# Twenty column chunks of x's projections, computed in pairs by Strassen's product in a dense stage ahead of the mixers; first branch projection woven with the memory attention

## The chip, the cores and the metric

The kernel runs on one core of one Trainium2 chip. The metric is the device time of one execution in microseconds (us). A profile is one execution recorded by the hardware profiler; its engines are PE (TensorE matmul), PEld (TensorE weight load), DVE (VectorE), ACT (ScalarE), POOL (GpSimd) and SP (SyncE, which issues most DMAs).

## The reference, cut to what matters

One residual block over 1024 tokens of width 1024, everything in f32:

```python
h = rmsnorm(x, norm_mix_g)
hq, hf, hi, hg, fq, fk, fv, ff, mq, gate_logits = split(h @ w_in)
y_a = hgrn2_mixer(hq, hf, hi, hg)            # 4 heads x 128, chunkwise recurrence
y_b = fox_mixer(fq, fk, fv, ff)              # 8 heads x 64, causal attention with forget bias
y_c = memory_mixer(mq, rmsnorm(mem) @ mem_kv_w)   # 4 heads x 128, 256 memory tokens
g = sigmoid(gate_logits)                     # 3 branches x 1024 channels
merged = g[0] * (y_a @ w_br_hgrn) + g[1] * (y_b @ w_br_fox) + g[2] * (y_c @ w_br_mem)
x = x + merged @ w_out
x = x + conv_glu_ffn(rmsnorm(x))             # 2 x 2816 wide up, 1024 down
```

## The kernel before, in words

Activations lie channel-major: 128 channels on the partitions, 1024 tokens along the free axis, eight such k-blocks for width 1024. Every f32 matrix product is made of three fp32r matmuls (`mm3`, lines 109 to 111): each operand is split into a high part and a low part (`split`: an ACT cast, line 115, or a POOL cast, line 119, and a DVE subtraction, line 123), and high*high, high*low and low*high are added up in PSUM.

A **chunk** is 128 output columns of one of x's projections: `cm_chunk` loads a 128x1024 weight tile (`raw`, line 134, on SP's queue, two buffers), splits it, and runs for each half of the tokens 8 k-blocks x 3 matmuls of 128x512, 48 matmuls in all. The stationary operand is the weight tile, the moving one uh/ul, the two parts of x times the norm gain. Of these chunks there are 12 for the recurrence (hq, hf, hg; three a head, `hgrn_prep`), 4 for the memory queries (`mem_prep`, line 799) and 24 for the merge gates. A gate chunk is evicted by `gate`: a DVE multiply by the norm factor rx (line 373), an ACT tanh (line 374) and a store to a DRAM tile `gd` (line 388), from which the branch stage loads it again.

The order of the work:

1. Start: x and mem come in, uh/ul are made, the memory keys and values and the first two gate chunks are computed while x arrives.
2. `fox_values`, `fox_proj(0)`: token-major projections, matmuls of 128x256.
3. Attention (fox): passes p = 0 to 3 of two heads each. `weave` interleaves a head's steps (`ahead` gives them priority 300) with `fox_proj(p+1)` and with gate chunks, by the list `NGF` (13 in all); in pass 3 the filler is `hgrn_values`. `fox_prep` (line 475 on) transposes the next pass's queries and keys. The attention itself: two matmuls for the logits (lines 521, 522), a DVE pass that adds the bias and takes the maximum (527), exp on ACT (537), a reciprocal on DVE (538), a scaling on POOL (539), transposes on PE (550 to 553), a split, two matmuls (562, 563).
4. Recurrence (hgrn): `hgrn_prep(0)` alone, then `hgrn_mix(h)` woven with `hgrn_prep(h+1)` and gate chunks by `NG[0:4]` = 1, 1, 0, 3.
5. Memory attention: `mem_prep(0)` alone, then `mem_attn(h)` woven with `mem_prep(h+1)` and gate chunks by `NG[4:8]` = 0, 0, 0, 3.
6. Branches 1, 0, 2 (`gates`, `br_chunk`): eight chunks of 24 matmuls each; then w_out, then the ConvGLU, whose up-projection already goes by Strassen's product (`unit`: two chunks of 128 columns by seven block products of 4 k-blocks x 3 matmuls, 84 matmuls) and the down-projection likewise.

The order on each engine is fixed before the run by the framework's scheduler, which lists instructions by priority and by its own estimate of when their inputs are ready; on the chip each engine then runs its list in order.

Of the kernel before, what the change touches and what calls it, by code (L numbers as in the profile page):

```python
# [14 lines left out]
P = 128  # L15
# [18 lines left out]
FOX_LATE, MEM_LATE = 0.2, 0.3  # L34
# [31 lines left out]
def tile_block(ctx: ExitStack, tc: tile.TileContext, xT, memT, vec, fbias, mats, hmask, w_cm, w_hi, w_fqk, w_fv,  # L66
               w_mkv, w_br, w_out, w_up, w_dn, outT):
# [101 lines left out]
    order = [(br, j) for br in (1, 0, 2) for j in range(8)]  # L169
# [195 lines left out]
    gd = tc.dram_tile([NPRE, 2, P, HB], F32, name="gd")  # L365

    def gate_chunk(br, j):
        for n, ps in cm_chunk(w_cm[16 + 8 * br + j], KC, uh, ul):
            yield n, gate(n, ps)

    def gate(n, ps):
        gt = gp.tile([P, HB], F32, tag="gt", name="gt", bufs=3)
        V.tensor_mul(gt, ps, rx[:, n * HB:(n + 1) * HB])
        S.activation(gt, gt, AF.Tanh, scale=0.5)
        return gt
# [4 lines left out]
    early = iter(range(2, NPRE))  # L380

    def gates_early(count):
        for _ in range(count):
            i = next(early, None)
            if i is None:
                return
            for n, gt in gate_chunk(*order[i]):
                SP.dma_start(gd[i, n], gt)
                yield
# [215 lines left out]
    def hgrn_prep(h):  # L605
        ph = state["ph"]
        qt = ph.tile([P, T], F32, tag="hq", name=f"hq_{h}", bufs=2)
        at = ph.tile([P, T], F32, tag="ha", name=f"ha_{h}", bufs=2)
        gz = ph.tile([P, T], F32, tag="hz", name=f"hz_{h}", bufs=2)
        for what, base, dst in ((0, 4, at), (1, 0, qt), (2, 8, gz)):  # L610
            for n, ps in cm_chunk(w_cm[base + h], KC, uh, ul):
                sl = slice(n * HB, (n + 1) * HB)
                zt = ph.tile([P, HB], F32, tag="zt", name="zt")
                V.tensor_mul(zt, ps, rx[:, sl])
                d = dst[:, sl]
                S.activation(d, zt, AF.Tanh, scale=0.5)
                if what == 0:

                    G.tensor_scalar(d, d, TMIN, c1[:, h:h + 1], ALU.max, ALU.mult)
                else:  # L620

                    V.scalar_tensor_tensor(out=d, in0=d, scalar=1.0, in1=zt, op0=ALU.add, op1=ALU.mult)
                yield
        hset[h] = (qt, at, gz)

# [147 lines left out]
    yc = pyc.tile([P, 4, T], F32, tag="y16", name="yc")  # L773
    mkh = pm.tile([P, 4, NM], F32R, tag="mkh", name="mkh")
# [3 lines left out]
    mkf = pm.tile([P, 4, NM], F32, tag="mqh", name="mkf2", bufs=2)  # L778
    mvf = pm.tile([P, 2, HB], F32, tag="mql", name="mvf2", bufs=2)
    SP.dma_start(mkf.rearrange("p a b -> p (a b)"), kvd[:, 0, :])  # L780
    SP.dma_start(mvf.rearrange("p a b -> p (a b)"), kvd[:, 1, :])
    split(G, mkh, mkl, mkf)
    split(G, mvh, mvl, mvf)

    pyb = tc.alloc_tile_pool(name="pyb", bufs=1, side="left", reuse_waits="tile")
    yb = pyb.tile([P, 4, T], F32, tag="y16", name="yb")
    SP.dma_start(yb, ybd)
# [3 lines left out]
    def mem_prep(h):  # L791
        mqh = pm.tile([P, T], F32R, tag="mqh", name=f"mqh_{h}", bufs=2)
        mql = pm.tile([P, T], F32R, tag="mql", name=f"mql_{h}", bufs=2)
        rq = pm.tile([P, 8], F32, tag="rq", name=f"rq_{h}", bufs=2)
        prs = ps_tr()
        for n, ps in cm_chunk(w_cm[12 + h], KC, uh, ul):
            sl = slice(n * HB, (n + 1) * HB)
            sq = pm.tile([P, HB], F32, tag="msq2", name="msq2")
            S.activation(sq, ps, AF.Square)
            split(S, mqh[:, sl], mql[:, sl], ps)  # L800
# [3 lines left out]
            yield  # L804
# [4 lines left out]
        mset[h] = (mqh, mql, rq)  # L809

# [42 lines left out]
    wsplit[:] = [S, V]  # L853


    yts = {0: ya, 1: yb, 2: yc}

    spots = (("mqh", 2), ("mql", 2), ("mqh", 2), ("mql", 2), ("mkh", 1), ("mkl", 1), ("mvh", 1), ("mvl", 1))
    ys = [pm.tile([P, T], F32R, tag=t, name=f"y{i}", bufs=b) for i, (t, b) in enumerate(spots)]
    yh, yl = ys[0::2], ys[1::2]  # L860
    spots = (("msq2", 1), ("mpt", 3), ("mpt", 3), ("mpt", 3), ("mph", 2), ("mph", 2), ("mpl", 2), ("mpl", 2))
    mg0 = [pm.tile([P, HB], F32R if t in ("mph", "mpl") else F32, tag=t, name=f"mg0_{i}", bufs=b)
           for i, (t, b) in enumerate(spots)]
    mg1 = []

    def merged(j, n):
        return mg0[2 * j + n].bitcast(F32) if j < 4 else mg1[0][:, j - 4, n * HB:(n + 1) * HB]

    def br_chunk(br, j):


        wh, wl = weights(w_br[br, j], (4, P))
        half = [slice(n * HB, (n + 1) * HB) for n in range(2)]
        if j in (0, 7):
            get = ps_lg if j else ps_tr
            ps = [get(), get()]
# [11 lines left out]
    def gates():  # L888
        for i, (br, j) in enumerate(order):
            y = yts[br]  # L890
            gts = []
            if i < NPRE:
                for n in range(2):
                    gt = gp.tile([P, HB], F32, tag="gt", name="gt", bufs=3)
                    SP.dma_start(gt, gd[i, n])
                    gts.append(gt)
            else:
                gts = [gt for _, gt in gate_chunk(br, j)]
            if j == 0:
                for c in range(4):  # L900
                    split(S, yh[c], yl[c], y[:, c, :])
            if i == 4:
                mg1.append(pyb.tile([P, 4, T], F32, tag="y16", name="mg1"))
            for n, ps in br_chunk(br, j):
# [8 lines left out]
    run_all(gates())  # L913
    mh, ml = both_parts("m")
    for j in range(8):
        for n in range(2):
# [3 lines left out]
    pyb.release()  # L920
# [6 lines left out]

    pr = tc.alloc_tile_pool(name="pr", bufs=1, side="right", reuse_waits="tile")
    fam = {}

    def new_family(pool, name):
        fam[name] = [pool.tile([P, 4, HB], F32R, tag=f"{name}{p}", name=f"{name}{p}") for p in "hl"]

# [12 lines left out]
    def family_block(name, k, src):  # L946
        h, l = fam[name]
        return split(S, h[:, k, :], l[:, k, :], src)

# [5 lines left out]

    late = {}
# [77 lines left out]

    def product(ps, op, b, first):
        wh, wl = op
        bh, bl = fam[b]
        for k in range(4):
            ks = slice(k * P, (k + 1) * P)
            mm3(ps, wh[:, ks], wl[:, ks], bh[:, k, :], bl[:, k, :], first and k == 0, k == 3, not first)  # L1040
# [258 lines left out]
def _layout(inp):  # L1299
# [48 lines left out]
    o["w_cm"] = chunks(np.concatenate([hq, hf, hg, mq, gt], axis=1))  # L1348
# [44 lines left out]
```

## Time and profile before

| what | us |
|---|---|
| three runs, median (lowest to highest) | 1778.5 (1777.14 to 1780.22) |
| the profiled execution's own time | 1779.33 |
| its span, first to last instruction | 1777.6 |
| attention (fox) in the trace, first logits to last output | about 143.6 to 508 |
| recurrence (hgrn) | about 508 to 787 |
| memory attention | about 787 to 891 |
| branches and w_out | about 891 to 1123 |
| ConvGLU up, then down | about 1123 to 1554, then to the end |

The busy times of an engine are unions of its instructions' times. A matmul's recorded duration is its latency, about 400 ns for a 128x512 one, while successive ones start about 230 ns apart: a PE that is busy all the time may still run at full rate or not, and the rate is read from the number of matmuls in a stretch.

### The profile page before, as it was taken

How to read it: one execution, taken by the hardware profiler on the slowest of the kernel's cores; microseconds unless marked ns; L12 is line 12 of the kernel's file. 1: busy time of each engine (PE TensorE's matmuls, PEld its weight loads, DVE VectorE, ACT ScalarE, POOL GpSimd, SP SyncE). 2: the span in 40 equal slices, each digit the busy share in tenths (PEclk: the TensorE clock that was granted, in tenths of full speed). 3: DMA queues.
4: the chain of work that ended last, by engine and by line, in shares of the span. 5: the costliest groups of instructions: out<-in, count | busy, mean ns of one | idle time of the engine just before them, and what ended most of it. 6: DMA issues, size and time to landing. Idle time of an engine off the chain costs nothing.

```text
span 1777.6 us, 24366 instructions
## 1 busy us (share of the span) xinstructions
PE 1755.8 (99%) x9173; PEld 1487.1 (84%) x9173; DVE 1146.1 (64%) x2070; ACT 731.0 (41%) x1215; POOL 359.9 (20%) x430
## 2 busy tenths in 40 slices
PE   7999999999999999999999999999999999999999
PEld 5899899889988888888888888788888888778887
DVE  8436665565657778735446665787877877775654
ACT  4336454444544344314521143543433444433332
POOL 5214334342223333323100000111111111100000
PEclk9999999999999999999999999999999999999999
DMA  7212221221211111130144442455545444394782
GB/s 265 98 61 70 70 69 62 73 88 60 69 50 43 42 48 34 45 125 25 54 142 142 148 166 84 142 165 173 154 132 158 124 125 140 135 371 144 232 281 83
DMA packets 75573, 208.45 MB, mean 117 GB/s; under 512 B 8752, under 2 KB 11576, under 8 KB 75328
## 3 DMA queue, kind: packets, MB, share of 16 engines
q1 hardware_dynamic: 60864, 154.99, 25.2%
q0 software_dynamic: 14592, 51.91, 10.3%
q8 instruction: 72, 1.18, 0.3%
q14 instruction: 45, 0.37, 0.1%
HBM read 168.82 MB, written 61.12 MB: 129 GB/s over the span
## 4 chain that ended last, share of the span: by engine, by line
PE 96%; issue 1%; DMA 1%; DVE 1%; POOL 1%; ACT 0%; SPq 0%; DVEq 0%; POOLq 0%
PE pp L110 21%; PE pp L111 21%; PE pp L109 21%; PE lg L110 4%; PE lg L111 4%; PE lg L109 4%; PE tr L109 2%; PE tr L110 2%; PE tr L111 2%; PE lg L696 2%; PE po L563 1%; PE lg L522 1%; PE po L562 1%; PE lg L521 1%; PE po L110 1%
## 5 line engine op out<-in xcount | busy, mean ns | idle before, releaser
L111 PE MATMUL pp<-uh,wl 128*128 128x512 f32 x608 | 243.6, 401 | 0.0
L110 PE MATMUL pp<-ul,wh 128*128 128x512 f32 x608 | 243.2, 400 | 0.0
L109 PE MATMUL pp<-uh,wh 128*128 128x512 f32 x608 | 241.7, 397 | 0.0
L110 PE MATMUL pp<-wl,uh 128*128 128x256 f32 (+1 forms) x512 | 144.9, 283 | 0.0
L111 PE MATMUL pp<-wh,ul 128*128 128x256 f32 (+1 forms) x512 | 144.6, 283 | 0.0
L109 PE MATMUL pp<-wh,uh 128*128 128x256 f32 (+1 forms) x512 | 143.9, 283 | 0.0
L115 ACT CAST wh<-raw 128x1024 fp32r<-128x1024 f32 (+2 forms) x80 | 73.1, 914 | 153.0 <-PE pp L110 123.3
L109 PEld LDWEIGHTS pp<-uh,wh 128*128 128x128 f32 x608 | 115.3, 190 | 23.3
L110 PEld LDWEIGHTS pp<-ul,wh 128*128 128x128 f32 x608 | 114.5, 188 | 22.9
L111 PEld LDWEIGHTS pp<-uh,wl 128*128 128x128 f32 x608 | 114.4, 188 | 22.5
L1074 POOL DMA_DIRECT2D rw<-in_w_up x44 | 24.3, 559 | 463.8 <-DVE wl L123 410.8
L123 DVE TENSOR_TENSOR wl<-raw,wh 128x1024 fp32r<-128x1024 f32 (+2 forms) x87 | 93.9, 1081 | 29.7 <-ACT wh L115 23.0
L115 ACT CAST wh<-s 128x512 fp32r<-128x512 f32 x85 | 51.9, 619 | 125.6 <-PE pp L110 60.7
L110 PEld LDWEIGHTS pp<-wl,uh 128*128 128x128 f32 x512 | 96.4, 188 | 0.9
L111 PEld LDWEIGHTS pp<-wh,ul 128*128 128x128 f32 x512 | 96.5, 189 | 0.6
L109 PEld LDWEIGHTS pp<-wh,uh 128*128 128x128 f32 x512 | 96.2, 189 | 0.7
L115 ACT CAST dwh<-wr 128x1024 fp32r<-128x1024 f32 (+1 forms) x42 | 41.1, 980 | 124.7 <-PE tr L110 41.7
L115 ACT CAST wh<-rw 128x512 fp32r<-128x512 f32 x65 | 40.0, 620 | 86.1 <-PE pp L110 48.3
L123 DVE TENSOR_TENSOR dwl<-wr,dwh 128x1024 fp32r<-128x1024 f32 (+1 forms) x42 | 47.6, 1133 | 38.7 <-ACT dwh L115 37.5
L677 POOL TENSOR_TENSOR X<-X,kt 128x256 f32<-128x256 f32 x48 | 48.2, 1011 | 109.9 <-ACT X L676 109.9
L539 POOL TENSOR_SCALAR pt<-pt,st 128x128 f32<-128x128 f32 (+3 forms) x64 | 57.0, 891 | 62.4 <-DVE st L538 50.5
L537 ACT ACTIVATE pt<-pt,st 128x128 f32<-128x128 f32 (+3 forms) x64 | 49.7, 777 | 35.1 <-DVE st L534 29.0
(426 smaller groups left out, 4845.1 us busy)
## 6 DMA issues: line engine op xcount, KB each, us to landing
rw<-in_w_up POOLq DMA_DIRECT2D x44, 512.0 KB, 4.7
raw<-in_w_cm SPq DMA_DIRECT2D x40, 512.0 KB, 3.5
sd<-in_w_dn POOLq DMA_DIRECT2D x30, 512.0 KB, 6.1
br<-yd SPq DMA_DIRECT2D x30, 512.0 KB, 5.4
gd<-gt SPq DMA_DIRECT2D x46, 256.0 KB, 2.0
gt<-gd SPq DMA_DIRECT2D x46, 256.0 KB, 2.7
yd<-fc SPq DMA_DIRECT2D x44, 256.0 KB, 2.1
wr<-sd SPq DMA_DIRECT2D x20, 512.0 KB, 4.5
```

The costliest lines, as they stand in the source:

```text
L109: PE.matmul(ps, lh, rh, start=first, stop=False, skip_group_check=more)
L110: PE.matmul(ps, lh, rl, start=False, stop=False, skip_group_check=more)
L111: PE.matmul(ps, ll, rh, start=False, stop=last, skip_group_check=more)
L115: S.copy(out, in_)
L123: return (sub or V).tensor_sub(l, src, h.bitcast(F32))
L521: PE.matmul(ps[:, :w], qa[i][:, tsl], kh[i][:, s0:s0 + w], start=True, stop=False)
L522: fox_sets[p][3] = PE.matmul(ps[:, :w], qa[i][:, tsl], kl[i][:, s0:s0 + w], start=False, stop=True)
L537: S.activation(pt[:, :ns], pt[:, :ns], AF.Exp, bias=st[:, 2:3], accum_out=st[:, 3:4])
L539: G.tensor_scalar(pt[:, :ns], pt[:, :ns], st[:, 3:4], 0.0, ALU.mult, ALU.add)
L677: G.tensor_mul(Xk, Xk, Kv[:, :, 0, :])
L696: PE.matmul(o[:, b * 64:(b + 1) * 64], X[:, b * P:(b + 1) * P], Xq[:, b * bpb:(b + 1) * bpb, :], start=True, stop=True)
L1074: late["raw"] = G.dma_start(raw[:, 2 * i:2 * i + 2, :], src[:, 2 * i:2 * i + 2, :])
```

## The change: what it does

Ten **pairs** of chunks leave the mixers and are computed between the start and `fox_values`, each by seven products of half-size blocks instead of eight: (hf0, hq0), (hg0, a gate), the four memory-query chunks in two pairs, and twelve further gates in six pairs. That is the whole of `hgrn_prep(0)`, all of the projections of `mem_prep`, and 13 gate chunks. Two gate chunks (`NCOVER`) run ahead of them in the plain way. Three gate chunks stay with the attention, one each in passes 0 to 2; four stay with the recurrence (`NG` = 0, 1, 0, 3), none with the memory attention.

The Strassen blocks T1 to T4 are sums and differences of quarters of x, so x is read from memory a second time (`differences`, on POOL's DMA queue), scaled on ACT, and combined and split on DVE and ACT. The weights of a pair come in four quarters from a new input `w_pair` on POOL's queue. What the pairs give goes to DRAM tiles (`gd`, `hd`, `mqd`) and is loaded where it is used: `hgrn_load` takes the place of `hgrn_prep(0)`, and `mem_prep` loads its queries instead of projecting them.

The first branch (branch 1, the attention's) is woven with the memory attention; its input, the parts of y_b, lies in the tiles of uh/ul, which the last gate chunk, now run k-block by k-block, frees. Each branch's merged sums lie in other tiles than before.

```diff
-NGF = [0, 3, 1, 2, 0, 5, 2, 0]
-NG = [1, 1, 0, 3, 0, 0, 0, 3]
-NPRE = 2 + sum(NG) + sum(NGF)
+ORDER = [(br, j) for br in (1, 0, 2) for j in range(8)]
+NCOVER = 2
+NPAIR = 13
+NG = [0, 1, 0, 3]
+_dense = [4, 0, 8, 16 + 8 * ORDER[4][0] + ORDER[4][1], 12, 13, 14, 15]
+_dense += [16 + 8 * br + j for br, j in ORDER[5:4 + NPAIR]]
+PAIRS = list(zip(_dense[0::2], _dense[1::2]))
...
+    def product(ps, op, b, first):
+        wh, wl = op
+        for k in range(4):
+            ks = slice(k * P, (k + 1) * P)
+            bh, bl = block(b, k)
+            mm3(ps, wh[:, ks], wl[:, ks], bh, bl, first and k == 0, k == 3, not first)
...
+    def dense_unit(src, put, first, families):
+        raw = []
+        whole = None if first else dense.raw()
+        for i in range(2):
...
+            with tc.issue_after(late["rows"].ins):
+                G.dma_start(t, src[:, 2 * i:2 * i + 2, :])
+            raw += [t[:, 0, :], t[:, 1, :]]
+        a11, a21, a22, a12 = raw
+        x, y = ps_proj(), ps_lg()
+        o1 = dense.operand(a11)
...
+        product(x, o1, "B11", True)
+        e1 = dense.snap(x)
+        if first:
+            z = ps_tr()
+            product(z, o6, "B21", True)
+            put(0, 0, z, e1)
+            next(families)
+        product(y, o2, "T1", True)
+        e5 = dense.snap(y)
+        product(x, dense.operand(s2), "T2", False)
+        e2 = dense.snap(x)
+        run_all(families)
+        s4 = dense.sum_of(4, s2, a12)
+        product(y, dense.operand(s4), "B22", False)
+        put(0, 1, y, e2)
+        s3 = dense.sum_of(3, a11, a21)
+        product(x, dense.operand(s3), "T3", False)
+        put(1, 1, x, e5)
...
+        product(x, dense.operand(a22), "T4", False)
+        put(1, 0, x, None)
...
+    rows = [ps1.tile([P, 4, HB], F32, tag=t, name=f"xr{t}") for t in ("T4h", "T4l")]
+    rows += [dense.raw() for _ in range(2)]
...
+    def differences():
+        b = []
+        for k, t in enumerate(rows):
+            t = t.rearrange("p (c n) t -> p c (n t)", c=2)
+            for c in range(2):
+                late["rows"] = G.dma_start(t[:, c, :], xT[:, k + 4 * c, :])
+            for c in range(2):
+                S.activation(t[:, c, :], t[:, c, :], AF.Copy, scale=col(C_GX + k + 4 * c))
+            b.append([t[:, c, n * HB:(n + 1) * HB] for c in range(2) for n in range(2)])
+        for k, (b11, b12, b21, b22) in enumerate(b):
+            V.tensor_sub(b11, b11, b12)
+            family_block("T1", k, b11)
+        yield
...
+    wsplit[:] = [S, V]
+    cover, families = gates_early(NCOVER), differences()
+    next(cover)
+    next(families)
+    run_all(cover)
+    next(families)
+    small_consts()
+    for i, chunks_of in enumerate(PAIRS):
+        dense_unit(w_pair[i], dense_put(chunks_of), i == 0, families)
+    ps1.release()
...
-    wsplit[:] = [S, V]
     run_all(fox_values())
-    small_consts()
     run_all(fox_proj(0))
     fox_prep(0)
     for p in range(3):
-        weave((ahead(fox_attn(p, 0), AHEAD), FOX_STEPS), (fox_proj(p + 1), 8),
-              (gates_early(NGF[2 * p]), 2 * NGF[2 * p], FOX_LATE))
+        heads = chain(fox_attn(p, 0), fox_attn(p, 1))
+        filler = chain(fox_proj(p + 1), gates_early(1))
+        weave((ahead(islice(heads, 32), AHEAD), 32), (islice(filler, 8), 8))
         fox_prep(p + 1, fox_sets[p][3])
-        weave((ahead(fox_attn(p, 1), AHEAD), FOX_STEPS),
-              (gates_early(NGF[2 * p + 1]), 2 * NGF[2 * p + 1], FOX_LATE))
+        weave((ahead(heads, AHEAD), 12), (filler, 2))
...
-        weave((ahead(fox_attn(3, i), AHEAD), FOX_STEPS), (islice(values, 8), 8),
-              (gates_early(NGF[6 + i]), 2 * NGF[6 + i], FOX_LATE))
+        weave((ahead(fox_attn(3, i), AHEAD), FOX_STEPS), (islice(values, 8), 8))
...
-    run_all(hgrn_prep(0))
+    hgrn_load()
     for h in range(3):
         weave((ahead(hgrn_mix(h, ya), AHEAD), HGRN_STEPS), (hgrn_prep(h + 1), 6), (gates_early(NG[h]), 2 * NG[h]))
-    weave((ahead(hgrn_mix(3, ya), AHEAD), HGRN_STEPS), (gates_early(NG[3]), 2 * NG[3]))
+    weave((ahead(hgrn_mix(3, ya), AHEAD), HGRN_STEPS), (gates_early(NG[3], True), 2 * NG[3]))
...
+    yh, yl = [[place(p, 2 + c, f"y{p}{c}") for c in range(4)] for p in "hl"]
+    for c in range(4):
+        t = place("hl"[c % 2], c // 2, f"yb{c}", F32)
+        SP.dma_start(t, ybd[:, c, :])
+        split(S, yh[c], yl[c], t)
...
-        for n, ps in cm_chunk(w_cm[12 + h], KC, uh, ul):
+        SP.dma_start(t, mqd[h])
...
-    wsplit[0] = G
-    run_all(mem_prep(0))
-    for h in range(3):
-        weave((mem_attn(h), MEM_STEPS), (mem_prep(h + 1), 2), (gates_early(NG[4 + h]), 2 * NG[4 + h], MEM_LATE))
-    weave((mem_attn(3), MEM_STEPS), (gates_early(NG[7]), 2 * NG[7], MEM_LATE))
...
+    weave((memory(), 4 * MEM_STEPS), (branch(1, yh, yl), 16))
+    for c in range(4):
+        split(S, yh[c], yl[c], ya[:, c, :])
+    run_all(branch(0, yh, yl))
...
+    run_all(branch(2, ys[0::2], ys[1::2]))
```

`dense_put` evicts a product: for a gate a DVE addition where two products are summed, a DVE multiply by rx, an ACT tanh and a store to `gd`; for the recurrence's three chunks the same and a further operation on POOL or DVE, stored to `hd`; for a memory query a copy or addition, stored to `mqd`.

More of the change, by code (lines that the diff above doesn't have):

```diff
@@ L166, in cm_chunk @@
             yield n, ps
-    order = [(br, j) for br in (1, 0, 2) for j in range(8)]
+    order = ORDER
     pu = tc.alloc_tile_pool(name="pu", bufs=1, side="left")
@@ L363, in tile_block, with gate_tile @@
     ybd = tc.dram_tile([P, 4, T], F32, name="ybd")
[L365 to L369, printed above, removed]
+    gd = tc.dram_tile([len(order), 2, P, HB], F32, name="gd")
+    hd = tc.dram_tile([3, P, T], F32, name="hd")
+    mqd = tc.dram_tile([4, P, T], F32, name="mqd")
+    def gate_tile():
+        return gp.tile([P, HB], F32, tag="gt", name="gt", bufs=3)
     def gate(n, ps):
-        gt = gp.tile([P, HB], F32, tag="gt", name="gt", bufs=3)
+        gt = gate_tile()
         V.tensor_mul(gt, ps, rx[:, n * HB:(n + 1) * HB])
@@ new lines, in tile_block, with new_family, family_block, block @@
+    ps1 = tc.alloc_tile_pool(name="ps1", bufs=1, side="right", reuse_waits="tile")
+    late = {}
+    fam = {}
+    def new_family(pool, name):
+        fam[name] = [pool.tile([P, 4, HB], F32R, tag=f"{name}{p}", name=f"{name}{p}") for p in "hl"]
+    def family_block(name, k, src):
+        h, l = fam[name]
+        return split(S, h[:, k, :], l[:, k, :], src)
+    def block(b, k):
+        if b in fam:
+            return [t[:, k, :] for t in fam[b]]
+        c, n = int(b[1]) - 1, int(b[2]) - 1
+        return [t[k + 4 * c][:, n * HB:(n + 1) * HB] for t in (uh, ul)]
@@ new lines, in tile_block @@
+    dense = Dense()
+    def dense_unit(src, put, first, families):
[3 more added lines that the diff above has]
+            if first:
+                t = wp.tile([P, 4 * 264], F32, tag="raw", name="raw", bufs=2)[:, :2 * HB]
+                t = t.rearrange("p (a b) -> p a b", a=2)
+            else:
+                t = whole[:, 2 * i:2 * i + 2, :]
+            with tc.issue_after(late["rows"].ins):
[4 more added lines that the diff above has]
+        o1 = dense.operand(a11)
+        if first:
+            o6 = dense.operand(a12)
+        s1 = dense.sum_of(1, a21, a22)
+        o2 = dense.operand(s1)
+        s2 = dense.sum_of(2, s1, a11)
+        product(x, o1, "B11", True)
+        e1 = dense.snap(x)
+        if first:
+            z = ps_tr()
[13 more added lines that the diff above has]
+        put(1, 1, x, e5)
+        if not first:
+            z = ps_tr()
+            product(z, dense.operand(a12), "B21", True)
+            put(0, 0, z, e1)
+        product(x, dense.operand(a22), "T4", False)
+        put(1, 0, x, None)
@@ L777, in tile_block @@
     mvl = pm.tile([P, 2, HB], F32R, tag="mvl", name="mvl")
[L778 to L787, printed above, removed]
+    for h, l, w in ((mkh, mkl, 0), (mvh, mvl, 1)):
+        t = pm.tile([P, T], F32, tag="mqf", name=f"mkv{w}", bufs=2)
+        SP.dma_start(t, kvd[:, w, :])
+        split(G, h, l, t.rearrange("p (a b) -> p a b", a=h.shape[1]))
     mset = {}
@@ L809, in mem_prep @@
         mset[h] = (mqh, mql, rq)
+        yield
     def mem_attn(h):
@@ L886, in br_chunk, with branch @@
                 yield n, ps
-    def gates():
-        for i, (br, j) in enumerate(order):
-            y = yts[br]
+    def branch(br, yh, yl):
+        for j in range(8):
+            i = order.index((br, j))
             gts = []
[L892 to L904, printed above, removed]
+            for n in range(2):
+                gt = gate_tile()
+                SP.dma_start(gt, gd[i, n])
+                gts.append(gt)
+            for n, ps in br_chunk(br, j, yh, yl):
                 dst = merged(j, n)
@@ L911, in gates, with memory @@
                 yield
-    run_all(gates())
-    mh, ml = both_parts("m")
+    def memory():
+        run_all(mem_prep(0))
+        yield
+        for h in range(4):
+            if h < 3:
+                run_all(mem_prep(h + 1))
+            yield from mem_attn(h)
+    weave((memory(), 4 * MEM_STEPS), (branch(1, yh, yl), 16))
+    for c in range(4):
+        split(S, yh[c], yl[c], ya[:, c, :])
+    run_all(branch(0, yh, yl))
+    spots = (("mqh", 2), ("mql", 2), ("mqh", 2), ("mql", 2), ("mkh", 1), ("mkl", 1), ("mvh", 1), ("mvl", 1))
+    ys = [pm.tile([P, T], F32R, tag=t, name=f"yc{i}", bufs=b) for i, (t, b) in enumerate(spots)]
+    for c in range(4):
+        split(S, ys[2 * c], ys[2 * c + 1], yc[:, c, :])
+    run_all(branch(2, ys[0::2], ys[1::2]))
+    mh, ml = [], []
     for j in range(8):
+        k = (2, 3, 4, 5, 6, 7, 0, 1)[j]
+        mh.append(place("h", k, f"mh{j}"))
+        ml.append(place("l", k, f"ml{j}"))
         for n in range(2):
@@ L1033, in snap @@
         return e
[L1035 to L1040, printed above, removed]
     def first_products(o1, o2, o3, between=None):
```

149 lines of the change are left out of this document (112 added, 37 removed).

## The prediction

> **What bounds the kernel now.** I read the page's first two parts first, then the busy times by stretch, because a PE that is busy 99% of the time need not run at full rate.
>
> ```profile
> span 1777.6 us, 24366 instructions
> PE 1755.8 (99%) x9173; PEld 1487.1 (84%) x9173; DVE 1146.1 (64%) x2070; ACT 731.0 (41%) x1215; POOL 359.9 (20%) x430
> PEclk9999999999999999999999999999999999999999
> ```
>
> PE has work from end to end at a full clock, DVE 64%. The busy times by stretch give the rate; the columns are the stretch and its length, then busy time and number of instructions of PE, PEld, DVE, ACT, POOL, then clock, DMA share and GB/s.
>
> ```profile
> 143.60:508.00 364.40, 364.40 (x2397) 331.18 (x2397) 219.03 (x654) 186.59 (x362) 129.65 (x168) 1.00 0.20 67
> 508.00:787.00 279.00, 279.00 (x1546) 236.32 (x1545) 200.21 (x388) 108.18 (x190) 93.14 (x84) 1.00 0.13 46
> 545.00:720.00 175.00, 175.00 (x1001) 149.21 (x999) 136.44 (x270) 72.33 (x126) 62.42 (x58) 1.00 0.12 40
> 787.00:891.00 104.00, 104.00 (x564) 88.44 (x563) 48.89 (x107) 47.28 (x115) 28.14 (x41) 1.00 0.21 74
> 1170.00:1500.00 330.00, 330.00 (x1428) 267.78 (x1427) 254.50 (x381) 132.41 (x203) 44.66 (x72) 1.00 0.50 147
> 90.00:110.00 20.00, 20.00 (x167) 20.00 (x166) 4.27 (x10) 3.86 (x8) 1.15 (x2) 1.00 0.16 54
> 700.00:730.00 30.00, 30.00 (x174) 25.64 (x173) 26.35 (x53) 11.32 (x22) 10.94 (x11) 1.00 0.10 36
> ```
>
> Row 5 is the ConvGLU's up-projection, which already goes by Strassen units: 1428 matmuls of 128x512 in 330 us, **231 ns** each. Row 6 is a stretch of 128x256 matmuls: 20/167 = 120 ns. So the kernel is bound by the number of matmuls PE starts. DVE's share in the attention (row 1) is 219/364 = 60%, in the recurrence (row 2) 200/279 = 72%: PE carries the slack there, filled with gate and query chunks.
>
> **What the change removes.** A chunk has 48 matmuls, so it costs PE 48 x 0.231 = 11.1 us. A pair has 96 before and 7 x 4 x 3 = 84 after; ten pairs save 120 matmuls, 120 x 0.231 = **27.7 us**. No other matmul goes or comes. Everything else in the change can only decide how much of this arrives.
>
> **The dense units in their steady state: nothing lost.** A unit has 84 x 0.231 = 19.4 us of PE. Beside it DVE has seven operand subtractions, four sums and some seven operations at the put, 18 at 0.69 us (rows below): 12.4 us, 64%. Row 5 is the same product scheme at a DVE share of 254.5/330 = 77% and keeps the full rate. The weights come on POOL's queue as there, where a load of 512 KB lands in 4.7 us; two make a unit, and POOL has only these queued in that stage apart from one clamp at each half of the first pair.
>
> ```profile
> L123 DVE TENSOR_TENSOR wl<-rw,wh x65: 680/685/695, 1138.0 to 1544.2; 128x512 fp32r<-128x512 f32 x65
> L1066 DVE TENSOR_TENSOR s<-rw x43: 683/689/697, 1131.8 to 1522.1; 128x512 f32<-128x512 f32 x43
> rw<-in_w_up POOLq DMA_DIRECT2D x44, 512.0 KB, 4.7
> L267 ACT ACTIVATE xk<-xk x7: 1057/1062/1067, 26.6 to 56.0; 128x1024 f32<-128x1024 f32 x7
> 66.17 0.28 PE L109 MATMUL pp<-wh,uh 128*128 128x256 f32 x1
> ```
>
> **The dense stage's start: +5 us (0 to 12).** PE is free for it at 66.2 (last row). Two cover gates and the products B11 and B21 last 22.2 + 5.5 us, so T1 is due at 94, T2 at 97, T3 at 102, T4 at 105. The second read of x lands in tiles that held x, whose last square is done at 57 (fourth row). 4.2 MB take about 18 us at the 234 GB/s of the start:
>
> ```profile
> 57.00:66.00 9.00, 9.00 (x49) 7.58 (x48) 3.77 (x5) 3.31 (x6) 1.65 (x1) 1.00 0.68 234
> 1110.00:1141.00 31.00, 28.40 (x135) 23.78 (x134) 19.39 (x33) 19.75 (x36) 5.44 (x8) 0.96 0.33 119
> 1137.38 0.51 PE L109 MATMUL pp<-T3h,wh 128*128 128x512 f32 x1 [2.60 <-ACT wh L115]
> 1561.08 0.50 PE L110 MATMUL pp<-dbl,dwh 128*128 128x512 f32 x1 [1.53 <-DVE dbl L123]
> ...
> 1561.88 0.61 PE L110 MATMUL pp<-dbl,dwh 128*128 128x512 f32 x1
> ...
> 1565.27 0.41 PE L111 MATMUL pp<-dbh,dwl 128*128 128x512 f32 x1
> ```
>
> that is 75, and 94 leaves time for the scaling (eight of about 1.1 us on ACT). But from 57 to 105 DVE has 16 differences, 16 splits and the first unit's own 18 operations, 50 x 0.69 = 35 us, and two gates: 40 us in 48. The second unit's weights wait for a tile that holds x's rows until T4 is split, and then 4.7 us for the landing. The nearest row is the ConvGLU's own first unit, which makes its blocks the same way: PE waits 2.60 us there (third row), 28.4 us busy in 31, and comes back slowly. I take +5; nothing if the scheduler's order keeps ahead; 12 if rows and second weights are each a landing late.
>
> The last three rows bear on what a wait costs: after a wait of 1.53 us eight matmuls start between 1561.88 and 1565.27, 0.42 us apart, which is 8 x 0.19 = 1.5 us on top of the wait. [...]
>
> **The attention with less cover: +5 us (0 to 14).** Ten chunks leave it. The rows that carry its DVE work:
>
> ```profile
> L123 DVE TENSOR_TENSOR wl<-raw,wh 128x1024 fp32r<-128x1024 f32 x25 | 31.4, 1256 | 7.6 <-ACT wh L115 7.5
> L373 DVE TENSOR_TENSOR gt<-pp,rx 128x512 f32<-128x512 f32 x26 | 17.9, 689 | 30.1 <-PE pp L111 30.1
> L481 DVE SCALAR_TENSOR_TENSOR kl<-tr,cv,kh 64x512 fp32r<-64x512 f32 x16 | 11.9, 747 | 9.1 <-ACT kh L480 8.9
> L538 DVE RECIPROCAL st<-st 128x1 f32<-128x1 f32 x64 | 10.3, 161 | 32.6 <-ACT pt L537 32.5
> L459 DVE TENSOR_TENSOR z<-z,fr 128x1024 f32<-128x1024 f32 x8 | 10.1, 1257 | 3.5 <-POOL fr L128 3.5
> L457 DVE TENSOR_REDUCE fr<-fsq 128x16 f32<-128x1024 f32 x7 | 8.5, 1214 | 1.3 <-ACT fsq L456 1.2
> ```
>
> PE: 364.4 - 10 x 11.1 = 253 us. Pass 3 keeps its 384 token-major matmuls, 46 us; passes 0 to 2 have 192 each (69 us together), three gates (33) and transposes (about 5); 100 us are left for attention proper, 25 a pass. So passes 0 to 2 are 182 us of PE. DVE: a chunk costs 1.26 + 2 x 0.69 = 2.6 us, so 219 - 26 = 193; per pass 0 to 2 the projection and preparation take 2 x 1.26 + 2 x 1.26 + 2 x 1.21 + 8 x 0.75 + one chunk = 16 us, pass 3's weights 5; 140 are left for attention, 35 a pass. Passes 0 to 2: 48 + 105 = **153 us of DVE beside 182 of PE, 84%**. That is no excess, but DVE works its list in order and stands 0.5 us at each of 64 reciprocals for ACT's exp (fourth row); where PE has no chunk to fill such a hole, PE waits as well. Waits of DVE for PE itself (30.1 us behind gates, second row) go with the chunks.
>
> **The recurrence with less cover: +3 us (0 to 15).** Five chunks leave the stretch 508 to 787 (hgrn_prep(0)'s three, a gate, mem_prep(0)'s): 279 - 55.5 = 223.5 us of PE. DVE loses 2.6 for each of four chunks and at most 4 x 0.88 at line 622, 14 in all:
>
> ```profile
> L614 DVE TENSOR_TENSOR zt<-pp,rx 128x512 f32<-128x512 f32 x24 | 16.5, 686 | 8.2 <-PE pp L111 7.9
> L622 DVE SCALAR_TENSOR_TENSOR hz<-hz,zt 128x512 f32<-128x512 f32 x8 | 7.1, 882 | 0.4 <-ACT hz L616 0.4
> nf<-negFd SPq DMA_DIRECT2D x8, 512.0 KB, 3.8
> ```
>
> 200 - 14 = 186 of 223.5, **83%**. What is known: over 175 us (row 545 to 720) DVE ran at 136.4/175 = 78%, and over 30 us at 26.35/30 = 88%, PE busy throughout. I take it that 82% can be kept up, between the two rows: then the attention's three passes last 153/0.82 = 187 us instead of 182 and the recurrence 186/0.82 = 227 instead of 223.5, **+8** together. Both ends: nothing at 84% or more; at 78% 196 and 238.5, +29.
>
> hgrn_prep(0) no longer stands between attention and recurrence; its results are loaded (three of 512 KB; the last row's load of that size on SP's queue takes 3.8 us). hgrn_prep(1)'s 33 us of matmuls cover that and the chain ahead of the recurrence's first matmul; without that cover it would cost the landing and that chain, some 15 us.
>
> **Memory attention and branch 1: +1 us (0 to 6).** Six chunks go (-67), branch 1's 192 matmuls come (+44): 104 - 22 = 82 us of PE, no longer after it. DVE: 48.9 less three gates (8), plus 16 puts, 8 weight and 4 larger splits (21): 62, 76%. Behind the loads of y_b, which wait on SP for tiles that the last gate frees, stand the loads of keys, queries and branch weights; that chunk lasts 11.1 us and frees a k-block each 1.4, so they go out before PE needs them. If not, one landing and one split are late, about 6 us.
>
> At nothing: about 11 MB more of DMA (x's rows 4.2, hd and mqd written and read 7), since the shares above are 0.13 to 0.21 outside start and ConvGLU; stores of 256 KB on SP in place of the same for gates; the merged sums' other places; w_out, ConvGLU.
>
> **Sum.** Against the profiled execution (1779.3, its span 1777.6 and 1.7 around it): 1779.3 - 27.7 + 5 + 5 + 3 + 1 = 1765.6. The median of the runs shown is 0.8 lower: **1765 us**.
>
> **Rivals.**
> 1. *The full gain*: DVE keeps up 84% and the start's waits replace waits of the same size. For it: row 700 to 730, and that PE has no wait to show in either mixer now. 1778.5 - 27.7 + 1 = 1752.
> 2. *DVE becomes the bound of the mixers* (slower): its in-order list holds no more than the 78% of row 545 to 720. 1778.5 - 27.7 + 6 + 29 = 1786. It decides from a share of (153 + 186)/(405.5 + 21.7) = 0.794 downwards, where the mixers lose what is left of the gain. For it: nothing here shows DVE above 78% for long. Against: at 78% DVE's waits were mostly for a full PE, so it isn't a ceiling.
> 3. *The clock falls too*: as 2, with one wait of over 2.6 us at the end of each of 8 heads and 4 recurrence heads, each with 1.5 us of half rate: 1786 + 18 = 1804. Against it: in 143 to 787 the clock is 1.00 throughout.
>
> **Chances.** Forecast (1757 to 1775) 0.47; rival 1 (1749 to 1757) 0.21; upper ends in one or two stages that just eat the gain 0.10; rival 2 0.16; rival 3 0.06. A measurement of this kernel tells 0.2%, 3.5 us, from no change: faster 0.68, same 0.10, slower 0.22. The range leaves out the lower part of rival 1 and the upper part of rivals 2 and 3: 1751 to 1788.
>
> **What would show it.** Right: 120 matmuls fewer; ten dense units of 19 to 20 us each between about 88 and 290; a DVE share near 82% in the attention's first three passes and the recurrence; few waits of PE there. Wrong: PE idle and a clock under 1 in the mixers (rivals 2, 3); waits of PE for DMA or DVE at the second unit beyond 12 us; or a gap between the recurrence's end and branch 1's first product, where I put only 1 us.

## The result and the profile after

The changed kernel takes 1824.3 us (1822.5 to 1825.6) against 1779.4 us for the kernel before in the same session: ratio **1.0254** (95% interval 1.0236 to 1.0271), 45 us slower. I had forecast 1765, range 1751 to 1788.

The first parts of its page:

```profile
span 1823.8 us, 24498 instructions
PE 1766.0 (97%) x9053; PEld 1483.9 (81%) x9053; DVE 1222.8 (67%) x2218; ACT 792.3 (43%) x1324; POOL 366.7 (20%) x451
PEclk9899999999999899999999999999999999999999
```

9173 matmuls have become 9053: the 120 are gone as forecast. But PE now sits idle for 1823.8 - 1766.0 = 57.8 us where it was 21.8, and the row of the clock is no longer all nines after the start. The stretches of the changed kernel (columns as in the prediction):

```profile
57.00:120.00 63.00, 53.59 (x213) 41.83 (x212) 34.99 (x58) 29.23 (x47) 10.39 (x15) 0.89 0.47 171
110.00:300.00 190.00, 190.00 (x830) 153.98 (x829) 109.83 (x174) 73.85 (x130) 14.42 (x20) 1.00 0.31 107
372.00:681.00 309.00, 290.59 (x2021) 266.88 (x2019) 198.79 (x632) 169.50 (x339) 130.40 (x172) 0.96 0.17 52
480.00:510.00 30.00, 24.07 (x142) 19.48 (x141) 23.25 (x84) 17.57 (x38) 16.80 (x19) 0.89 0.10 29
510.00:570.00 60.00, 60.00 (x455) 57.37 (x454) 35.84 (x109) 31.68 (x65) 25.60 (x35) 1.00 0.20 59
570.00:630.00 60.00, 52.12 (x362) 47.79 (x362) 41.38 (x138) 34.35 (x69) 28.84 (x38) 0.89 0.14 39
660.00:705.00 45.00, 37.48 (x169) 30.61 (x168) 28.55 (x61) 22.04 (x34) 15.45 (x13) 0.86 0.23 76
705.00:930.00 225.00, 225.00 (x1283) 190.86 (x1283) 176.56 (x357) 91.28 (x165) 71.60 (x68) 1.00 0.20 64
930.00:960.00 30.00, 26.10 (x123) 21.16 (x122) 18.30 (x25) 11.04 (x17) 3.10 (x3) 0.89 0.44 134
1020.00:1045.00 25.00, 21.91 (x106) 16.54 (x105) 14.52 (x30) 15.29 (x36) 6.31 (x11) 0.93 0.00 1
```

Read each row for two losses: the length less PE's busy time, and the length times what the clock lacks.

| place | idle | clock | together |
|---|---|---|---|
| the dense stage's start, 57 to 120 | 9.4 | 0.11 x 63 = 6.9 | 16 |
| the attention, 372 to 681 | 18.4 | 0.04 x 309 = 12.4 | 31 |
| the rest of the entry into the recurrence, to 705 | about 3 | about 2 | 5 |
| the recurrence's end, 930 to 960 | 3.9 | 3.3 | 7 |
| the memory attention's end, 1020 to 1045 | 3.1 | 1.8 | 5 |

Together 64 us. The second loss runs partly through the first, so this is a rough sum, but it is most of the 45 + 27.7 = 73 us that have to be explained. The rest lies in pieces too short for such rows, or outside them. Two stages do what was forecast: the dense units (second row: 830 matmuls in 190 us, 229 ns each, a full rate), and the recurrence once it runs (eighth row: DVE 176.6/225 = 78%, PE without a gap, clock 1.00).

For the attention there is a second count, by its matmuls. From its first logits to the last store of its output the kernel before takes 363.8 us (143.6 to 507.4) and the change 303.7 us (377.5 to 681.2), with 422 fewer 128x512 matmuls recorded in between. At 231 ns these are 97.5 us, so 266.3 us were due, and **37 us** are lost there. The expectation of no_scale below goes by this count; with it 70 of the 73 us are placed.

What happened at the start is in the order of time. First the kernel before, then the changed one; a row gives the start, the duration of the issue, and in brackets the idle time before it and what ended that.

```profile
68.04 0.34 SPq L278 DMA_DIRECT2D rx_d<-rx_row  x1
69.27 0.34 SPq L279 DMA_DIRECT2D rx<-rx_d  x1
...
73.10 1.29 DVE L373 TENSOR_TENSOR gt<-lg,rx 128x512 f32<-128x512 f32 x2 [10.65 <-DMA rx<-rx_d]
```

```profile
65.54 0.56 POOL L551 DMA_DIRECT2D xrT4h<-in_xT  x1
66.09 1.07 POOL L551 DMA_DIRECT2D xrT4l<-in_xT  x2
67.15 2.12 POOL L551 DMA_DIRECT2D rw<-in_xT  x4
69.28 0.54 POOL L466 DMA_DIRECT2D raw<-in_w_pair  x1
...
69.99 0.34 SPq L285 DMA_DIRECT2D rx_d<-rx_row  x1
75.24 0.34 SPq L286 DMA_DIRECT2D rx<-rx_d  x1
81.99 1.29 DVE L381 TENSOR_TENSOR gt<-lg,rx 128x512 f32<-128x512 f32 x2 [18.86 <-DMA rx<-rx_d]
...
82.72 1.23 ACT L382 ACTIVATE gt<-gt 128x512 f32<-128x512 f32 x2 [12.76 <-DVE gt L381]
83.85 1.13 ACT L553 ACTIVATE xrT4h<-xrT4h,cv 128x1024 f32<-128x1024 f32 x1
83.93 0.79 PE L116 MATMUL pp<-uh,wh 128*128 128x512 f32 x1 [5.64 <-DVE gt L381]
```

The norm factor rx makes its way through DRAM in two transfers, a store of 4 KB and a load that spreads it (512 KB). Before, the load could be issued 1.2 us after the store, landed in 3.7 us, and rx was used at 73.1. Now the second read's eight transfers of 512 KB (the first was issued at 64.81, ahead of these rows) and a weight load have been issued ahead of the store; the load follows 5.2 us after it and lands in 6.7 us, and rx is used at 82.0. Two things wait for it: the gates' products, which hold PSUM banks (last row: PE waits 5.64 us for DVE's line 381), and, on ACT's list, the scaling of the rows behind the gates' tanh, from 83.85 on.

In the attention, the chain of work through a stretch without cover shows what PE waits for; a row gives the start, the duration, the engine, the tile and the line.

```profile
484.92 3.79 DMA nf<-negFd
...
489.72 0.47 POOL nfm L714
...
490.65 0.47 PE lg L719
...
496.33 0.42 DVE pt L725
...
498.27 0.72 ACT pt L735 x2
499.01 0.16 DVE st L736
```

From 488.75 on the work passes from engine to engine, in pieces of mostly under a microsecond, and no engine is full: DVE has 23.25 us of work in these 30 (row 480 to 510). I read the stretch as lasting as long as the blocks' chains. The first row is part of that chain, too: the load of a head's forget bias, 3.79 us, into a tile with a single buffer. No run took it out, so its share of the loss is not known.

Into the recurrence the same view has one long piece, the load of what the pairs computed for its first head:

```profile
683.33 6.42 DMA ha<-hd
```

It is issued behind the attention's last store (681.17) and lands at 689.75. The prediction had 3.8 us for such a load.

### The profile page after: what moved, and what is told of

It is laid out like the page before. It is cut to its first block, busy times and chain, and to the rows that moved or that the text cites. A ratio compares the mean times of both kernels' runs of the same rounds, so it can differ in the third digit from the quotient of the medians.

```text
span 1823.8 us, 24498 instructions
## 1 busy us (share of the span) xinstructions
PE 1766.0 (97%) x9053; PEld 1483.9 (81%) x9053; DVE 1222.8 (67%) x2218; ACT 792.3 (43%) x1324; POOL 366.7 (20%) x451
## 3 DMA queue, kind: packets, MB, share of 16 engines
q0 software_dynamic: 18624, 66.59, 12.7%
## 4 chain that ended last, share of the span: by engine, by line
PE 89%; DVE 3%; ACT 2%; DMA 2%; issue 2%; POOL 1%; SPq 0%; DVEq 0%; ACTq 0%; POOLq 0%
PE pp L117 19%; PE pp L118 19%; PE pp L116 19%; PE lg L116 4%; PE lg L117 4%; PE lg L118 4%; PE tr L118 2%; PE tr L116 2%; PE tr L117 2%; PE lg L899 2%; PE po L761 1%; PE po L760 1%; PE tr L748 1%; PE po L117 1%; PE po L116 1%
## 5 line engine op out<-in xcount | busy, mean ns | idle before, releaser
L122 ACT CAST wh<-s 128x512 fp32r<-128x512 f32 x125 | 75.4, 618 | 160.2 <-PE pp L117 72.7
L116 PE MATMUL pp<-uh,wh 128*128 128x512 f32 x328 | 133.9, 408 | 9.8 <-DVE gt L381 5.6
L118 PE MATMUL pp<-uh,wl 128*128 128x512 f32 x328 | 134.7, 411 | 0.0
L117 PE MATMUL pp<-ul,wh 128*128 128x512 f32 x328 | 133.6, 407 | 0.0
L130 DVE TENSOR_TENSOR wl<-raw,wh 128x1024 fp32r<-128x1024 f32 (+2 forms) x70 | 71.5, 1021 | 34.5 <-ACT wh L122 34.5
L130 DVE TENSOR_TENSOR wl<-s,wh 128x512 fp32r<-128x512 f32 x125 | 85.3, 685 | 7.6 <-ACT wh L122 7.6
L116 PEld LDWEIGHTS pp<-uh,wh 128*128 128x128 f32 x328 | 63.8, 194 | 23.9 <-DVE gt L381 6.3
L130 DVE TENSOR_TENSOR wl<-rw,wh 128x512 fp32r<-128x512 f32 x92 | 61.6, 685 | 32.1 <-PE pp L118 15.5
L118 PEld LDWEIGHTS pp<-uh,wl 128*128 128x128 f32 x328 | 63.4, 193 | 14.6 <-DVE wl L130 0.9
L117 PEld LDWEIGHTS pp<-ul,wh 128*128 128x128 f32 x328 | 63.6, 194 | 13.4
```

The source lines that it names most:

```text
L116: PE.matmul(ps, lh, rh, start=first, stop=False, skip_group_check=more)
L117: PE.matmul(ps, lh, rl, start=False, stop=False, skip_group_check=more)
L118: PE.matmul(ps, ll, rh, start=False, stop=last, skip_group_check=more)
L122: S.copy(out, in_)
L130: return (sub or V).tensor_sub(l, src, h.bitcast(F32))
```

## The experiments

"The change" is the changed kernel (1824.3 us, ratio 1.0254). Theory: the start's loss is rx standing behind the second read; the others are chains left without enough PE work beside them. Rivals: DVE's amount of work; the order in which the cover is used. The kernel before differs by up to 2 us between the sessions of these runs (1777.4 to 1779.4), so small differences are read from the ratios. What is said of places within a run comes from one profiled execution of each kernel.

**rx_by_pe**

```diff
-    spread_dma(rx, rt, p0, "rx")
+    spread(rx, rt)
```

> Edit: the norm factor rx is spread over the partitions by PE and an ACT copy instead of by a store and a load through DRAM. In the changed kernel the load of rx lands at about 82 us (it was in use at 73 before), behind the second read of x, and PE's gate products wait 5.6 us for a PSUM bank. Theory 'the queue of the second read delays rx': rx is ready at about 70, the first gap goes, 1816 us (6 to 9 less). Rival 'the second read and its scaling on ACT are the late part' (the scaled rows end at 97.5 us whatever rx does): the gap only moves behind the cover products, at most 3 us less, 1821 to 1824.

Measured: 1803.8 us, ratio 1.0146 (1.0131 to 1.0161), 20 us less than the change and more than either theory gave. From 57 to 90 us PE has no idle time and the clock is nearly full:

```profile
57.00:90.00 33.00, 33.00 (x157) 27.25 (x156) 18.84 (x31) 20.94 (x33) 7.13 (x11) 0.98 0.61 229
```

The scaling on ACT that the rival held to be late for itself starts at 71.4 instead of 83.8: it, too, had stood behind rx. The rival is out.

Only half of the 20 us is won at the start, though. The attention's first logits come 10.8 us earlier (366.7 instead of 377.5), the last store of its output 16.4 us (664.8 instead of 681.2), the last logits of the recurrence (line 899) 20.3 us (911.5 instead of 931.8). Some 6 us are won within the attention and 4 within the recurrence, where the edit changes nothing directly; why is not shown.

**rows_sp**

```diff
-                late["rows"] = G.dma_start(t[:, c, :], xT[:, k + 4 * c, :])
+                SP.dma_start(t[:, c, :], xT[:, k + 4 * c, :])
```

(the weights' loads lose the hold that named the rows' last issue)

> Edit: the second read of x is issued on SP's queue, behind the store and the load of rx, instead of on POOL's; rx still goes through DRAM. In the changed kernel eight reads of 512 KB and a weight load are issued from 65.5 us on, the store of rx at 70.0; it takes 5.2 us and the load lands at 82. Theory 'rx is late because it stands behind the second read in the DMA engines': rx lands near 74, the gates' evictions and the scaling behind them on ACT start early, and the reads are only a few us later: 1808 to 1816. Rival 'the way through DRAM is late for itself': 1822 to 1828.

Measured: 1815.1 us, ratio 1.0200 (1.0186 to 1.0214), 9 us less. The load of rx now follows its store after 1.3 us and rx is used at 75.8, but the rows are read later.

```profile
70.56 0.34 SPq L285 DMA_DIRECT2D rx_d<-rx_row  x1
71.83 0.34 SPq L286 DMA_DIRECT2D rx<-rx_d  x1
72.27 0.85 SPq L550 DMA_DIRECT2D xrT4h<-in_xT  x2
...
75.77 1.29 DVE L381 TENSOR_TENSOR gt<-lg,rx 128x512 f32<-128x512 f32 x2 [6.74 <-DMA rx<-rx_d]
```

So the way through DRAM was not slow for itself; what stood ahead of it made it late: 5.2 us from store to load behind POOL's reads in the change, 1.3 us ahead of the reads here. That the rows came on POOL's queue and rx on SP's did not keep them apart in the change.

**fox_nine_gates**

```diff
-NPAIR = 13
+NPAIR = 7
-        filler = chain(fox_proj(p + 1), gates_early(1))
+        filler = chain(fox_proj(p + 1), gates_early(3))
```

> Edit: six gate chunks (three pairs) go back into the attention's passes 0 to 2, three a pass instead of one; seven pairs are left in the dense stage. PE work rises by 3 x 2.8 = 8.3 us. PE loses about 46 us of starts in the attention of the changed kernel (372 to 681 us), about 11 in the kernel before. Theory 'too little cover, or cover used up too early, leaves the attention's chain bare': the bare stretches at 480 to 510 and 570 to 630 (30 us together) mostly go, 1800 to 1808. Rival 'DVE is the bound': the gates add 6 x 2.6 = 16 us of DVE work, nothing is won, 1830 or more.

Measured: 1796.8 us, ratio 1.0108 (1.0093 to 1.0123): 27.5 us less than the change (26 by the ratios), although PE has 8.3 us more to do and DVE, within the attention, 15 us more (209.6 us against 194.3 from first logits to last store). The attention starts 60 us earlier here, so the stretch in which the change had its two gaps holds other blocks; it is whole:

```profile
480.00:630.00 150.00, 150.00 (x1077) 140.48 (x1076) 90.60 (x283) 80.72 (x163) 56.08 (x77) 1.00 0.18 61
```

The whole attention takes 335.8 us (317.9 to 653.7), where 363.8 - 134 x 0.231 = 332.8 were due: 3 us are lost in place of 37. More work for DVE in the attention made it faster, so DVE's amount of work is out as the bound. What is left sits at the attention's end and at the entry into the recurrence, from 630 to 705 (PE busy 69.5 of 75 us, clock 0.95).

**gate_held**

```diff
-        weave((ahead(heads, AHEAD), 12), (filler, 2))
+        run_all(ahead(heads, AHEAD))
+        with tc.issue_after(fox_sets[p][3].ins):
+            run_all(filler)
```

> Edit: the one gate chunk of each of passes 0 to 2 is held on PE until the pass's last logits matmul, instead of running as soon as a slot is free. Same work. Theory 'the order: the cover is spent before the chain is bare, the total would do': up to 11 us less in each of the two passes whose end is bare, 1804 to 1812. Rival 'the total of the cover is too small, the chain is longer than PE's work': the gap moves to where the gate was, 1820 to 1828. Rival 'DVE is the bound': no change, 1824.

Measured: 1821.2 us, ratio 1.0249 (1.0232 to 1.0266), no change that can be told. The gaps have moved, among other places to the first pass, from which a gate was taken:

```profile
390.00:420.00 30.00, 25.59 (x146) 21.71 (x144) 21.52 (x77) 17.75 (x36) 12.82 (x18) 0.77 0.18 60
570.00:690.00 120.00, 119.66 (x827) 110.97 (x828) 64.54 (x193) 59.28 (x114) 35.82 (x50) 1.00 0.20 64
```

In the change PE has no idle time from 390 to 420; in return the end of the attention, where the gates are now held, is nearly whole. The time alone fits the rival 'DVE is the bound' just as well; what speaks against that one is fox_nine_gates. Holding the gates until the end doesn't help: the cover is too small in total.

**no_scale**

```diff
-                V.reciprocal(st[:, 3:4], st[:, 3:4])
-                G.tensor_scalar(pt[:, :ns], pt[:, :ns], st[:, 3:4], 0.0, ALU.mult, ALU.add)
```

> Edit, on the changed kernel: the attention's probabilities are not divided by their sum (64 reciprocals on DVE and 64 multiplies on POOL left out, so the attention's output is not normalized). No PE work and hardly any DVE work goes (64 x 0.16 = 10 us of 202), but each block's chain loses POOL's 0.9 us, the reciprocal and two hand-overs. Theory 'a bare stretch lasts as long as the chain': of the 37 us that the attention lost 12 to 25 come back, 1800 to 1812. Rival 'DVE's amount of work sets the bare stretches': 3 to 5 us, 1819 to 1822.

Measured: 1803.3 us, ratio 1.0137 (1.0122 to 1.0153), 21 us less. PE's work is the same, the chain is one POOL instruction and one reciprocal shorter, and the second gap shrinks from 7.9 us of idle time to 3.7:

```profile
570.00:630.00 60.00, 56.35 (x430) 52.83 (x429) 42.67 (x138) 39.06 (x81) 18.10 (x27) 0.97 0.15 45
```

From first logits to last store the attention takes 286.4 us instead of 303.7, so 17 of the 21 us are won there. DVE's work went down by 9 us within it and POOL's by 50, but POOL was not full either: 130/309 = 42% in the change, and 28.8 of 60 us in this gap. That leaves the chain's length as what a bare stretch goes by.

**mem_first**

```diff
-    weave((memory(), 4 * MEM_STEPS), (branch(1, yh, yl), 16))
+    weave((ahead(memory(), AHEAD), 4 * MEM_STEPS), (branch(1, yh, yl), 16))
```

> Edit: the memory attention gets the attention's priority (300) over the branch products it is woven with. In the changed kernel branches 1 and 0 are used up as cover by about 1030 us, and PE then waits for the memory attention's output (6.9 us of starts lost between 1020 and 1050). Theory 'the memory chain is served too late': it ends earlier, 1817 to 1820. Rival 'its start is what is late (loads, and the switch from the recurrence at 940 to 950)': nothing moves, 1822 to 1826.

Measured: 1825.1 us, ratio 1.0266 (1.0250 to 1.0281); both gaps stay as they were. Nothing was won, and it doesn't settle which of several chains the gaps follow.

**pe_nine**: `spread` for rx and the nine gates together.

> Edit: rx spread by PE, and three gate chunks a pass in the attention (seven pairs in the dense stage). Theory 'the two losses are separate': 1824 - 20 - 27.5 = 1776 to 1778, level with the kernel before. Rival 'the same loss was counted twice' (what is late at the start comes back in the attention): 1785 to 1795.

Measured: 1783.8 us, ratio 1.0030 (1.0020 to 1.0039), between the two. The two repairs overlap by 5 to 7 us, and the traces show where: with nine gates the attention takes 335.7 us with rx spread by PE and 335.8 without, so the 6 us that rx_by_pe won within the attention are not won again. Seven pairs save 7 x 12 x 0.231 = 19.4 us, and the kernel stands 5 us above the one before, so 24 us are still lost; 8 of them show at the attention's end and the entry into the recurrence:

```profile
300.00:620.00 320.00, 320.00 (x2199) 295.11 (x2199) 202.12 (x610) 174.00 (x339) 130.89 (x167) 1.00 0.20 68
620.00:690.00 70.00, 65.11 (x328) 53.86 (x328) 48.16 (x103) 31.87 (x50) 24.48 (x21) 0.95 0.18 60
```

**pe_nine_prep**: as pe_nine, and `hgrn_prep(0)` run plainly between attention and recurrence again, with five pairs left. One gate more also goes to the recurrence's first head (`NG` = 1, 1, 0, 3).

```diff
-_dense = [4, 0, 8, 16 + 8 * ORDER[4][0] + ORDER[4][1], 12, 13, 14, 15]
+_dense = [16 + 8 * ORDER[4][0] + ORDER[4][1], 12, 13, 14, 15]
-    hgrn_load()
+    run_all(hgrn_prep(0))
```

> Edit: rx spread by PE, three gate chunks a pass, and the recurrence's first three chunks computed plainly between attention and recurrence again, as before (five pairs left in the dense stage: the memory queries and six gates; five gates in the recurrence). PE work rises by 5.5 us over the same with seven pairs. Theory 'hgrn_prep(0) was cover: without it attention's tail and the recurrence's first chain run bare' (17 us of starts lost between 660 and 720): about 12 us come back, 1768 to 1772. Rival 'the tail is short of cover for another reason': 1781 to 1784.

Measured: 1776.6 us, ratio 0.9989 (0.9980 to 0.9998). That is 7 us less than pe_nine with 5.5 us more work for PE, so it brought back about 12.7 us, the 12 of the theory. The time lies outside both forecasts, since they counted from 1776 to 1778 for pe_nine and not from its 1783.8. The edit puts in three chunks and a gate and takes the late loads of `hgrn_load` away; this run alone doesn't tell cover from loads.

**pe_prep**: the same on the kernel with rx spread by PE alone.

> Edit: rx spread by PE, one gate chunk a pass as in the change, and the recurrence's first three chunks computed plainly between attention and recurrence (eight pairs left). Against the kernel with rx spread by PE alone (1804): PE work +5.5 us. Theory 'hgrn_prep(0) was cover': 12 us come back, 1796 to 1800. Rival 'it only moves': 1807 to 1810.

Measured: ratio 1.0154 (1.0139 to 1.0169), 1805.9 us, against 1.0146 without: level within the intervals, so about 4 of the 5.5 us of added work came back, not 12; the time lies between the two forecasts. (Here, too, one gate more goes to the recurrence.) The traces don't show that it only moved. From the attention's last store to the end it takes 1171.8 us against 1137.7 in rx_by_pe, 34 us more for four chunks, 44 us of PE: about 10 us came back there. But the attention, with its gaps left as they were and the same 1974 matmuls, takes 301.7 us instead of 298.1, and the dense stage gives up 37.6 us where two pairs are 38.8. Why the attention got longer is not shown.

**pe_twelve**: rx by PE, four gates in each of passes 0 to 2, `NG` = 1, 1, 0, 3, five pairs left.

> Edit: rx spread by PE, four gate chunks a pass and five in the recurrence; five pairs left in the dense stage. Two pairs less than with three a pass cost PE 5.5 us. Theory 'three a pass are enough cover': 1780 to 1783. Rival 'the attention is still short of cover at three a pass': 1770 to 1776.

Measured: **1776.0 us, ratio 0.9978** (0.9968 to 0.9988), faster than both kernels, by 0.2% against the one before. At three a pass the attention's end and the entry were still short of cover; with a fourth, and one gate more in the recurrence's first head, PE is whole there:

```profile
300.00:590.00 290.00, 290.00 (x1870) 262.18 (x1870) 180.87 (x550) 153.19 (x300) 108.97 (x144) 1.00 0.21 70
590.00:660.00 70.00, 70.00 (x452) 62.88 (x452) 42.37 (x89) 32.26 (x51) 20.05 (x19) 1.00 0.22 76
900.00:1020.00 120.00, 116.86 (x598) 96.22 (x598) 89.07 (x170) 59.43 (x131) 25.45 (x36) 0.99 0.33 106
```

This kernel keeps the loads of `hgrn_load`, has as many matmuls as pe_nine_prep (9128 recorded) and takes the same time within the intervals. So cover repairs the entry with the loads in place.

Five pairs save 13.9 us of PE and 3 us arrive. Some of the rest is in the last row, the memory attention with branch 1.

**pe_twelve_six**: as pe_twelve with three gates in the recurrence, all in its last head, and six pairs.

> Edit: as pe_twelve (rx spread by PE, four gates a pass), but the gates of the recurrence go down from five to three, all in its last head, and six pairs are in the dense stage. PE work 2.8 us less than with five pairs. Theory 'the recurrence has cover to spare once the attention keeps its own': 1773. Rival 'the recurrence's first heads run short': 1776 to 1782.

Measured: 1778.7 us, ratio 0.9997 (0.9988 to 1.0006). Against pe_twelve that is 3.4 us more by the ratios, though PE has 2.8 us less to do. The time is the rival's, but its profile, of the slowest of its eleven runs, doesn't show the place that the rival names. In the recurrence's first heads, 640 to 720, PE is busy 79.76 of 80 us at a clock of 0.98, and from 720 to 900 it has no idle time at a clock of 1.00. What is lost lies just behind the recurrence, in the last 30 us of this row:

```profile
700.00:930.00 230.00, 225.73 (x1265) 191.86 (x1264) 173.10 (x340) 88.75 (x162) 71.59 (x60) 0.99 0.26 84
```

The 4.3 us are two waits of the branches' products, 1.6 and 2.7 us long, which end at 902.8 and 912.0 when DVE has merged earlier products (lines 1092 and 1094). Why two gates less in the recurrence cost time there stays open.

## Why the prediction was wrong, point by point

- *The bound and the saving* were right: 120 matmuls, a full rate in the dense units, no loss there.
- *"The dense stage's start: +5 us (0 to 12)"* failed in size and place. I had weighed when the rows arrive and what DVE has to do; the 4.2 MB of reads I set only against their own due time, not against the small transfers they were moved ahead of. The table puts the loss at 16 us; sending rx another way gave back 20, 11 of them before the attention's first logits.
- *"The attention with less cover: +5 us (0 to 14)"* is the step that failed most. I took cover as an amount: 182 us of PE beside 153 of DVE, so at 84% DVE nothing is missing. DVE never came near: over the attention it ran at 198.8/309 = 64%. The attention's chain crosses PE, DVE, ACT and POOL several times for each block, and in a bare stretch no engine is full. I had named the waits at the reciprocal and that PE would then wait as well, and still priced them by DVE's share. What lasts is the chain of one block, and PE needs work beside it for as long. By the count of matmuls 37 us were lost where I had put 5; two more gates a pass took this down to 3.
- *"The recurrence with less cover: +3 us (0 to 15)"*: in its inside right, at 78% DVE. The sentence that failed is that hgrn_prep(1)'s matmuls cover the entry: around 660 to 705 PE loses 7.5 us idle and has a clock of 0.86, and hgrn_prep(0) with one gate, put back, was worth 12.7 us once the passes had their gates. That is near the 15 us that the prediction named for an entry without cover and left out of its sum.
- *"Memory attention and branch 1: +1 us (0 to 6)"*: about 12 by the table, at the two ends. This is read from the trace alone; the one run aimed at it moved nothing, and undoing that part alone was not tried. In rx_by_pe the first of the two ends is better (PE busy 27.9 of 30 us at a clock of 1.00, 914 to 944), for a reason not shown.
- *The rivals*: the slower side was named, but by DVE as the bound, which the runs refute, and the slowest rival stood at 1804, 20 us short. The clock of the third rival came true without DVE as the bound: in the gaps it was granted 0.86 to 0.93, and by the table it cost 26 us beside 38 of waits. I had given it 0.06 and tied it to waits of over 2.6 us. Its 1.5 us of half rate come from one place in the kernel before, where the granted clock is 0.50 (1561.88 to 1565.27, behind a wait of 1.53 us); that a wait has to be over 2.6 us was my estimate and not shown.

So the step that failed is the price of thinner cover, by DVE's share instead of by the length of the chain, and beside it the small transfers that the second read was put ahead of. Of the 64 us in the table, runs have shown the start's part, the attention's and the entry's. What the last two places hang on stays open.

## What to carry to other kernels

Work that fills PE while a long chain of small steps runs elsewhere is not spare: before it is moved into a dense stage, ask how long the chain lasts with nothing beside it, not whether some engine would be over-full. Count cover by the stretch, not by the stage, and don't add up repairs: here two of them overlapped in the attention. When a bulk read is put early, look for the small transfers that will stand behind it, on other engines' queues too: here rx's load could follow its store, both on SP's queue, after 1.3 us ahead of the reads and after 5.2 us behind reads on POOL's.

## What the runs showed of the hardware that I had not expected

In the change the granted clock was 0.89 in the stretch 570 to 630, though the longest single wait of PE there is 2.27 us, shorter than the 2.6 us of my third rival; from 601 to 606, behind the waits below, it was 0.50. Whether one wait or several in a row went with it is not told apart here. And the store of rx to DRAM, 4 KB, after which the load that needs it could be issued in 1.3 us in rows_sp, took 5.2 us in the change behind eight reads of 512 KB and a weight load.

```profile
591.68 0.50 PE L719 MATMUL lg<-kh,qa 128*128 128x512 f32 x1 [0.86 <-DVE st L725]
596.58 0.63 PE L673 MATMUL tr<-ident,z 128*128 128x128 f32 x4 [2.27 <-DVE kl L679]
599.54 1.11 PE L673 MATMUL tr<-ident,z 128*128 128x128 f32 x4 [0.99 <-DVE qa L685]
```
